# When an encoder kernel's weight sums are transferred: six spacings and one delay changed

## The chip, the cores and the metric

The kernel runs on one core of a Trainium2 chip. The metric is the device time of one execution in microseconds (us), given as the median of several runs. The core's engines each work through a queue of their own, in order: TensorE (PE in the profile; PEld is its weight loads) multiplies, VectorE (DVE) and ScalarE (ACT) work on elements, GpSimd (POOL) does small work and issues some DMAs, SyncE (SP) issues most of the DMAs. All DMAs of the core share 16 DMA engines.

## What is computed

Two encoder layers over 256 tokens and 16 meta tokens, 2048 channels, float32. Cut to what matters:

```python
for i in range(DEPTH):                                   # 2 layers
    proj = rmsnorm(x, norm_mix[i]) @ w_in[i]             # q | k | v | f | ga | gf
    a_br = attention(q, k, v) @ w_attn_br[i]
    fr = real(fft2(f, axes=(position, group channel)))   # 8 groups of 128 channels
    s_br = fr @ w_four[i]
    x = x + (sigmoid(ga) * a_br + sigmoid(gf) * s_br) @ w_out[i]
    up = rmsnorm(x, norm_ffn[i]) @ w_up[i]
    x = x + (silu(dwconv3(up[:, :D_FF])) * up[:, D_FF:]) @ w_down[i]
return x[:, 16:]
```

## The kernel before

**Weight blocks.** Weights come from memory in blocks of 512 KB (128 partitions, 4 x 256 columns). Each block is loaded by SP into one of four buffers `raw` (L244; six in the last layer's feed-forward), rounded by ACT into `wh` (L280), and the rest of the rounding is formed by DVE as `wl` (L283); `wh` and `wl` have three buffers each. A block takes 24 matmuls: for each of 8 column pieces wh by the high part of the activations, wh by the low part, wl by the high part (L352 to L354). In the first layer the Fourier branch's blocks are first folded by DVE into `wpm` (L271). The list `order` fixes the sequence of all blocks; `next_split` starts the loads some blocks ahead of use.

**Stages.** Per layer: projections f (first layer), k, v, q; in the last layer f comes folded, between the second and the third q group, with its own loop of 16 blocks (`folded_f`, matmuls at L822 to L826, tiles `ps_f`). Then the branches in two halves after `BRANCH_ORDER`: the gates ga0 to ga7 and gf0 to gf7 (4 blocks each), the Fourier products s0 to s7 and attention products a0 to a7 (2 blocks each). After each half comes a half of the output projection (`ps_o`, 16 blocks). Then the feed-forward: up (`ps_ug`, `ps_uv`) and down (`ps_d`).

**Weight sums.** In the last layer part of the up and of the down projection is computed with fewer matmuls, from sums and differences of weight blocks and of activations (`products`, L1390, 196 products of one block each, spread over the layer's 152 other blocks by the list `DUE`). The sums of weight blocks are made ahead, in DRAM, by DMAs that GpSimd issues: first a copy of 1 MB from one place to another (L539), then a second transfer of 1 MB that adds to it. These are 56 copies and 56 accumulating transfers, 112 in all, in a fixed order: the sums for the up projection (`fv`, 32 transfers), then those for the first and second set of the down projection (`ft`, 48 and 32). Within a set of n pairs the order is copy, copy, add, copy, add and so on to copy, add, add. Each transfer stands behind a small copy on GpSimd (`tick`, L538) that reads the `wl` made last, so that it can't start much ahead of the matmuls.

**Steps.** While blocks are multiplied, a function `step` is called four times a block (twice for a product's block, not in `folded_f`). It does two things: it counts down to the next weight-sum transfer, one every `slow[2]` steps (0: none), and it runs at most one pending small task from a list, each of which says for how many steps it then waits. `drain` runs everything in that list at once, whatever it still waits for.

```python
if not force and slow[1] and slow[2]:
    slow[0] -= 1
    if slow[0] <= 0:
        slow[0] = slow[2]
        if next(slow[1], None) is None:
            slow[1] = None
```

In steps the stages are: first layer from gf0 on, 160 for the first half of the branches, 64 for its output projection, 160 and 64 for the second, 1056 for the feed-forward; last layer 96 for k, v and q, 120 to the third gf (gf2), 104 for the rest of the first half, 64, 160 and 64, then 1000 for the feed-forward.

**The first Fourier projection.** The first layer's f groups run first: groups 0 and 1 together in 32 steps, group 2 in 16, then `drain`, then group 3. A task of norm sums runs beside them: sixteen squares from step 4 to step 28, the statistics at steps 32, 36, 40 and 42, and then `f_evac` of group 0 at step 45 and of group 1 at step 47. `f_evac` ends by putting `f_chan` of its group on the list (L636), whose small products are written to `ps_fa` (L652, L653).

**Who sets the order.** Within an engine the planner of the language orders instructions by the program's order and by when it reckons their inputs ready; where the code says so (`keep_in_program_order`, `manual_schedule`) the program's order holds. The ticks and transfers keep theirs.

Of the kernel before, what the change touches and what calls it, by code (L numbers as in the profile page):

```python
# [158 lines left out]
def encoder_kernel(ctx, tc, xT, params, consts, bmat, cfold, csign, w_fl, w_f64c, w_in, w_abr, w_four, w_f64, w_out, w_up, w_down, w_vn, w_dn, w_dt, out):  # L159
# [129 lines left out]
    def push(gen, wait=0):  # L289
        shadow.append([wait, gen])  # L290

    slow = [0, None, 0]
# [296 lines left out]
    for l in range(DEPTH):  # L589
        last = l == DEPTH - 1  # L590
# [5 lines left out]
        with tc.tile_pool(name=f"mix{l}", bufs=1) as mp:  # L596
# [17 lines left out]
            def rt(name):  # L614
                return mp.tile([P, 2, 2 * TH], F32, tag="r", name=name, bufs=7)[:, :, :T]
# [8 lines left out]
            def f_evac(i, ps):  # L624
                ft = rt("ft")
                for m in range(MG):
                    nc.vector.tensor_tensor(ft[:, m, :], ps[m][:, :T], rstdB, op=ALU.mult)
                g2 = slice(2 * i, 2 * i + 2)
                tt = nc.vector.tensor_tensor
                nc.vector.tensor_copy(E[:, g2, 0:1], ft[:, :, 0:1])  # L630
                tt(E[:, g2, 1:128], ft[:, :, 1:128], ft[:, :, 271:144:-1], op=ALU.add)
                tt(E[:, g2, 128:256], ft[:, :, 1:129], ft[:, :, 271:143:-1], op=ALU.subtract)
                tt(remE[:, g2, 0:8], ft[:, :, 128:136], ft[:, :, 144:136:-1], op=ALU.add)
                nc.vector.tensor_copy(remE[:, g2, 8:9], ft[:, :, 136:137])
                tt(remO[:, g2, 9:16], ft[:, :, 129:136], ft[:, :, 143:136:-1], op=ALU.subtract)
                push(f_chan(i), 11 if l == 0 and i == 1 else 8)  # L636

            def chan_out(i, pv):
                hh = o1[0][:, i]
# [514 lines left out]
            def gate(kind, i):  # L1154
                ps = group((l, kind, i), xr(lo), W)
                th = rt("th")
                boff = 2 * KT * l + (0 if kind == "ga" else KT)
                for m in range(MG):
                    u = th[:, m, lo:T]
                    nc.vector.tensor_tensor(u, ps[m][:, :W], rstdB[:, lo:T], op=ALU.mult)  # L1160
                    bcol = bgh[:, boff + 2 * i + m:boff + 2 * i + m + 1]
                    nc.scalar.activation(u, u, AF.Tanh, bias=bcol, scale=0.5)
                return th

            tha, thf, w64s = {}, {}, []
            for half in range(2):
                slow[2] = 0
                mH = mL = None
                for n_, (kind, i) in enumerate(BRANCH_ORDER[half]):
                    if half or n_ >= (8 if last else 4):  # L1170
                        slow[2] = 26 if last else 15
                    j = i - 4 * half
                    if kind == "ga":
                        tha[i] = gate("ga", i)
                    elif kind == "gf":
                        w64s.append(split_w64(l, i))
                        thf[i] = gate("gf", i)
                    elif kind == "s":
                        def s_evac(m, ps, th=thf[i]):
                            e, o = (mp.tile([P, TH], F32, tag=t, name=t) for t in ("se", "so"))  # L1180
                            for a, p_ in ((e, ps[0]), (o, ps[1])):
                                nc.scalar.copy(a, p_[:, TH:2 * TH])
                                nc.vector.tensor_tensor(a, p_[:, :TH], a, op=ALU.add)
                            sp = mp.tile([P, T], F32, tag="sp", name="sp", bufs=2)
                            nc.vector.tensor_tensor(sp[:, 0:TH], e, o, op=ALU.add)
                            nc.vector.tensor_tensor(sp[:, TH:T], e[:, T - TH:0:-1], o[:, T - TH:0:-1], op=ALU.subtract)
                            t_ = th[:, m, lo:T]
                            nc.vector.scalar_tensor_tensor(t_, t_, 1.0, sp[:, lo:T], op0=ALU.add, op1=ALU.mult)

                        four_group((l, "s", i), fr, x64, w64s.pop(0), s_evac)  # L1190
                    else:
                        if mH is None:
                            drain()
                            mHf = mp.tile([P, AHn], F32R, tag="aH", name="mH")
                            mLf = mp.tile([P, ALn], F32R, tag="aL", name="mL")
                            mH = mHf[:, :8 * T].rearrange("p (k t) -> p k t", k=8)
                            mL = mLf[:, :8 * T].rearrange("p (k t) -> p k t", k=8)
                        ps = group((l, "a", i), lambda kt: (qH[kt // 4][:, kt % 4, lo:T], qL[kt // 4][:, kt % 4, lo:T]), W)
                        for m in range(MG):
                            k = 2 * j + m  # L1200
                            t_, h_ = tha[i][:, m, lo:T], mH[:, k, lo:T]
                            nc.vector.scalar_tensor_tensor(t_, t_, 1.0, ps[m][:, :W], op0=ALU.add, op1=ALU.mult)
                            nc.vector.tensor_tensor(t_, t_, thf[i][:, m, lo:T], op=ALU.add)
                            nc.scalar.copy(h_, t_)
                            nc.vector.tensor_tensor(mL[:, k, lo:T], t_, h_.bitcast(F32), op=ALU.subtract)  # L1205
                slow[2] = 22 if last else 20 if half else 15
                for mg in range(8):
                    ps = group((l, "o", half, mg), lambda kt: (mH[:, kt, lo:T], mL[:, kt, lo:T]), W)
                    for m in range(MG):
                        mt = 2 * mg + m  # L1210
                        nc.vector.scalar_tensor_tensor(XT[:, mt, lo:T], ps[m][:, :W], 0.5, XT[:, mt, lo:T], op0=ALU.mult, op1=ALU.add)
                        if half == 1:
                            norm_in(mt, P_NF + l * KT)


        with tc.tile_pool(name=f"ffn{l}", bufs=1) as fp:
# [46 lines left out]
                            norm_in(mt, P_NM + (l + 1) * KT)  # L1263
                k0 += n
            if not last:
                slow[2] = 0

            if last:
                X0, X1 = 26, 32
# [102 lines left out]
                def products():  # L1372
                    late = []
                    until(hold, "tokens")
                    slow[2] = 45
                    make_ahead()
                    bank.extend([psum.tile([P, 512], F32, tag="aux", name=f"ps_p{i}{h}") for h in range(2)] for i in range(2))
                    for s_, p, q in PRODUCTS:
                        ps = bank[(p in (4, 2, 1)) ^ s_ % 2]
                        fresh = p in (0, 4, 1)  # L1380
                        wh, wl = (w.rearrange("p c m -> p (c m)") for w in next_split())
                        direct = s_ == 0 and p in plain
                        if direct:
                            k, h = plain[p]
                            a, b = xH[:, k + q, xt[h]], xL[:, k + q, xt[h]]
                        else:
                            a, b = made.pop((s_, p, q))
                        for x, w, first, end in ((a, wh, True, False), (b, wh, False, False), (a, wl, False, True)):
                            for h in range(2):
                                nc.tensor.matmul(ps[h], x, w[:, 512 * h:512 * h + 512], start=fresh and (s_, q) in BEGIN and first,  # L1390
                                                 stop=(s_, q) in END and end, skip_group_check=not fresh)
                            if not first:
                                step()
                                pump()
                        if not direct and units[used[0]][1][-1] == q:
                            used[0] += 1
                        make_ahead()
                        if late and q % 2 == 0:
                            hand_out(*late.pop(0))
                        if (s_, q) in END:  # L1400
                            while late:
                                hand_out(*late.pop(0))
                            t_, c, minus = {0: (0, 0, 0), 4: (1, 2, 0), 5: (0, 2, 1), 2: (0, 2, 0), 6: (1, 2, 1), 1: (0, 0, 0), 3: (1, 0, 0)}[p]
                            late += [(s_, p, t_, c + h, ps[h], minus) for h in range(2)]
                            if p in (0, 3) or s_ == 0 and p == 6:
                                while late:
                                    hand_out(*late.pop(0))
                        yield
                    assert not late

                slow[2] = 18
                st["products"] = products()
                st["pool"] = fp
                for i in UP_ORDER:
# [131 lines left out]
```

## Time and profile before

| | |
|---|---|
| median of 3 runs | 2542.79 us (2540.98 to 2543.11) |
| profiled execution | 2546.1 us |
| its span | 2544.3 us |
| granted TensorE clock, mean | 0.999 |
| TensorE busy | 2528.2 us |
| VectorE busy | 1825.0 us |
| ScalarE busy | 1319.8 us |
| DMA moved, mean | 660.69 MB, 260 GB/s |

The span runs from the first to the last instruction of one profiled execution; the execution's time adds what lies around it. Busy time is the time in which at least one instruction of an engine was in flight. Matmuls overlap, so a group of them can be slower than it should be without TensorE showing idle. A group's line gives the source line, engine, operation, the tiles written and read, the count, and the busy and mean times. In the views by stage each engine's busy time is followed by its count of instructions; the row ends in the granted clock, the DMA engines' share and GB/s. A window cut around one kind of tile counts the instructions that touch it, neighbours at its edges too.

### The profile page before, as it was taken

To read this page: it belongs to the slowest core of one execution; us is meant where nothing else is said; L and a number is where in the kernel's file an instruction comes from. 1 tells how busy PE (TensorE), PEld (TensorE's weight loads), DVE (VectorE), ACT (ScalarE), POOL (GpSimd) and SP (SyncE) were. 2 spreads that over 40 slices of the span, in tenths; PEclk is the share of its full clock that TensorE was granted. 3 is DMA by queue.
4 is the path that set the end of the run, shared out by engine and by line. 5 is a ranking of instruction groups with operands and counts; after the bars stand their busy time and mean duration, and the time that the engine had idled before them with its cause. 6 is when DMAs were issued, how large, how long until landed. Compare 5 with 4: busy or idle time off the path is not lost.

```text
span 2544.3 us, 47646 instructions
## 1 busy us (share of the span) xinstructions
PE 2528.2 (99%) x18992; PEld 2447.4 (96%) x18992; DVE 1825.0 (72%) x2889; ACT 1319.8 (52%) x1893; POOL 132.3 (5%) x265
## 2 busy tenths in 40 slices
PE   9999999999999999999999999999999999999999
PEld 8999999999999999999999999999988999888987
DVE  7687766776666556666558877666778778777788
ACT  5455434554444334444445555444676566656565
POOL 0000100000000000000000000000000000000000
PEclk9999999999999999999999999999999999999999
DMA  6546889989989998999875646887889888887787
GB/s 238 163 156 217 261 270 288 280 262 302 308 271 305 300 306 274 281 318 294 252 247 183 201 150 209 246 266 240 260 293 282 298 274 285 288 286 264 240 268 261
DMA packets 171215, 660.69 MB, mean 260 GB/s; under 512 B 19424, under 2 KB 24672, under 8 KB 170096
## 3 DMA queue, kind: packets, MB, share of 16 engines
q1 hardware_dynamic: 152528, 538.07, 61.3%
q0 software_dynamic: 17024, 117.45, 18.7%
q8 instruction: 149, 2.44, 0.4%
q10 hardware_dynamic: 1440, 2.13, 0.2%
q14 instruction: 74, 0.61, 0.1%
HBM read 635.91 MB, written 136.31 MB: 304 GB/s over the span
## 4 chain that ended last, share of the span: by engine, by line
PE 86%; DMA 2%; DVE 1%; ACT 1%; issue 0%; ACTq 0%; DVEq 0%
PE ps_p L1390 10%; PE ps_ug L353 7%; PE ps_ug L354 7%; PE ps_ug L352 7%; PE ps_uv L348 4%; PE ps_d L353 3%; PE ps_uv L353 3%; PE ps_d L352 3%; PE ps_uv L354 3%; PE ps_d L354 3%; PE ps_uv L352 3%; PE ps_o L353 2%; PE ps_o L354 2%; PE ps_o L352 2%; PE ps_uv L349 2%; PE ps_gf L354 2%
## 5 line engine op out<-in xcount | busy, mean ns | idle before, releaser
L283 DVE TENSOR_TENSOR wl<-raw,wh 128x1024 fp32r<-128x1024 f32 (+1 forms) x937 | 1129.7, 1217 | 567.5 <-ACT wh L280 559.5
L280 ACT CAST wh<-raw 128x1024 fp32r<-128x1024 f32 (+1 forms) x937 | 976.0, 1046 | 890.8 <-PE ps_ug L353 201.2
L353 PE MATMUL ps_ug<-xHL,wh 128*128 128x272 f32 (+1 forms) x1408 | 401.9, 285 | 0.0
L354 PE MATMUL ps_ug<-xHL,wl 128*128 128x272 f32 (+1 forms) x1408 | 401.4, 285 | 0.4 <-DVE wl L283 0.4
L352 PE MATMUL ps_ug<-xHL,wh 128*128 128x272 f32 (+1 forms) x1408 | 400.8, 285 | 0.0
L353 PEld LDWEIGHTS ps_ug<-xHL,wh 128*128 128x128 f32 x1408 | 264.7, 188 | 3.2
L352 PEld LDWEIGHTS ps_ug<-xHL,wh 128*128 128x128 f32 x1408 | 264.6, 188 | 3.2
L354 PEld LDWEIGHTS ps_ug<-xHL,wl 128*128 128x128 f32 x1408 | 264.7, 188 | 0.6 <-DVE wl L283 0.6
L353 PE MATMUL ps_uv<-xHL,wh 128*128 128x272 f32 x704 | 203.3, 289 | 0.0
L353 PE MATMUL ps_d<-gHL,wh 128*128 128x272 f32 x704 | 202.9, 288 | 0.0
L352 PE MATMUL ps_d<-gHL,wh 128*128 128x272 f32 x704 | 202.9, 288 | 0.0
L354 PE MATMUL ps_uv<-xHL,wl 128*128 128x272 f32 x704 | 202.6, 288 | 0.0
L352 PE MATMUL ps_uv<-xHL,wh 128*128 128x272 f32 x704 | 202.3, 287 | 0.0
L354 PE MATMUL ps_d<-gHL,wl 128*128 128x272 f32 x704 | 202.1, 287 | 0.0
L1390 PE MATMUL ps_p<-wh,opnd 128*128 128x512 f32 x688 | 187.8, 394 | 0.0
L348 PE MATMUL ps_uv<-xHL,wh 128*128 128x512 f32 x448 | 159.8, 395 | 0.0
L353 PE MATMUL ps_o<-mL,wh 128*128 128x272 f32 (+1 forms) x512 | 146.6, 286 | 1.3 <-DVE mL L1205 1.3
L352 PE MATMUL ps_ga<-xHL,wh 128*128 128x272 f32 (+1 forms) x512 | 147.8, 289 | 0.0
L352 PE MATMUL ps_gf<-xHL,wh 128*128 128x272 f32 (+1 forms) x512 | 146.9, 287 | 0.1
L354 PE MATMUL ps_gf<-xHL,wl 128*128 128x272 f32 (+1 forms) x512 | 146.0, 285 | 0.4 <-DVE wl L283 0.4
L353 PE MATMUL ps_ga<-xHL,wh 128*128 128x272 f32 (+1 forms) x512 | 146.1, 285 | 0.0
L353 PE MATMUL ps_gf<-xHL,wh 128*128 128x272 f32 (+1 forms) x512 | 146.1, 285 | 0.0
(372 smaller groups left out, 5871.4 us busy)
## 6 DMA issues: line engine op xcount, KB each, us to landing
raw<-in_w_up SPq DMA_DIRECT2D x320, 512.0 KB, 5.2
raw<-in_w_in SPq DMA_DIRECT2D x191, 512.0 KB, 4.2
raw<-in_w_down SPq DMA_DIRECT2D x88, 512.0 KB, 5.4
raw<-ft SPq DMA_DIRECT2D x80, 512.0 KB, 4.8
raw<-in_w_out SPq DMA_DIRECT2D x64, 512.0 KB, 5.6
ft<-in_w_dn POOLq DMA_DIRECT2D x30, 1024.0 KB, 12.0
raw<-in_w_dn SPq DMA_DIRECT2D x60, 512.0 KB, 4.7
raw<-in_w_abr SPq DMA_DIRECT2D x32, 512.0 KB, 4.8
```

Of the source, the lines that this page charges most:

```text
L280: nc.scalar.copy(h[:, a:b], r[:, a:b])
L283: nc.vector.tensor_tensor(lo[:, a:b], r[:, a:b], h[:, a:b].bitcast(F32), op=ALU.subtract)
L348: nc.tensor.matmul(o2, h[:, c, sl], ab, start=kt == 0, stop=False)
L349: nc.tensor.matmul(o, lo[:, c, sl], ab[:, 0, :], start=False, stop=kt == nk - 1)
L352: nc.tensor.matmul(o, h[:, c, sl], a, start=kt == 0, stop=False)
L353: nc.tensor.matmul(o, h[:, c, sl], b, start=False, stop=False)
L354: nc.tensor.matmul(o, lo[:, c, sl], a, start=False, stop=kt == nk - 1)
L1390: nc.tensor.matmul(ps[h], x, w[:, 512 * h:512 * h + 512], start=fresh and (s_, q) in BEGIN and first, stop=(s_, q) in END and end, skip_gr ...
```

## The change

The spacings `slow[2]` of the weight-sum transfers are set anew, and the wait of `f_chan` in the first layer is 10 steps for group 0 (8 before) and 13 for group 1 (11 before). By stage, the spacing in steps:

| stage | before | after |
|---|---|---|
| first layer, gf0 to the end of the first half, and its output projection | 15 | 32 |
| first layer, second half of the branches | 15 | 32 |
| its output projection and the first feed-forward | 20 | 19 |
| last layer, k to gf2 | none | 40 |
| last layer, rest of both halves of the branches | 26 | 26 |
| last layer, output projections | 22 | 28 |
| last feed-forward, to the first product | 18 | 28 |
| last feed-forward, from the first product | 45 | 38 |

```diff
-                push(f_chan(i), 11 if l == 0 and i == 1 else 8)
+                push(f_chan(i), (10, 13, 8, 8)[i] if l == 0 else 8)
...
             for half in range(2):
-                slow[2] = 0
+                slow[2] = (40 if half == 0 else 26) if last else 0 if half == 0 else 32
                 mH = mL = None
                 for n_, (kind, i) in enumerate(BRANCH_ORDER[half]):
-                    if half or n_ >= (8 if last else 4):
-                        slow[2] = 26 if last else 15
+                    if half == 0 and n_ == (8 if last else 4):
+                        slow[2] = 26 if last else 32
...
-                slow[2] = 22 if last else 20 if half else 15
+                slow[2] = 28 if last else 19 if half else 32
                 for mg in range(8):
...
             if not last:
-                slow[2] = 0
+                slow[2] = 40
...
                     until(hold, "tokens")
-                    slow[2] = 45
+                    slow[2] = 38
...
-                slow[2] = 18
+                slow[2] = 28
                 st["products"] = products()
```

## The prediction

> **What bounds the kernel now.** I read first the page's head and its busy line.
>
> ```profile
> span 2544.3 us, 47646 instructions
> PE 2528.2 (99%) x18992; PEld 2447.4 (96%) x18992; DVE 1825.0 (72%) x2889; ACT 1319.8 (52%) x1893; POOL 132.3 (5%) x265
> ```
>
> TensorE is busy for 2528.2 of 2544.3 us. The change takes no work from it, so all it can return is time in which TensorE waits. The next view, busy time by stage, says where that is.
>
> ```profile
> 250.00:310.00 60.00, 55.85 (x429) 54.85 (x428) 43.35 (x75) 26.09 (x40) 5.44 (x10) 0.97 0.87 264
> 560.00:1330.00 770.00, 770.00 (x6145) 770.00 (x6144) 477.49 (x697) 330.46 (x413) 47.21 (x103) 1.00 0.90 289
> 1420.00:1560.00 140.00, 140.00 (x1163) 138.63 (x1162) 112.09 (x267) 77.69 (x162) 3.83 (x4) 1.00 0.48 157
> 1700.00:1800.00 100.00, 98.70 (x825) 98.49 (x825) 67.09 (x108) 49.64 (x74) 4.66 (x10) 1.00 0.83 250
> 1850.00:1990.00 140.00, 139.29 (x824) 122.86 (x823) 109.93 (x135) 93.04 (x120) 6.31 (x10) 1.00 0.90 299
> 1990.00:2225.00 235.00, 235.00 (x1559) 215.70 (x1558) 188.23 (x252) 143.37 (x182) 11.41 (x16) 1.00 0.87 282
> ```
>
> After the stretch, its length and TensorE's busy time, the last three columns are granted clock, DMA share and GB/s. The idle sits in the first layer's branches (4.15 us at 250 to 310), with crumbs at 1700 (1.30) and 1850 (0.71). The first feed-forward (560 to 1330) has none, though its DMA engines are 0.90 busy.
>
> Busy time hides part of a loss, because overlapping matmuls fill in. So I set equal groups side by side: the attention products a0, a1, a2 and Fourier products s1, s3, s4 of the first layer, its gates gf5, gf6, and the last layer's two output projections.
>
> ```profile
> 250.60:256.80 6.20, 6.15 (x48) 6.04 (x48) 0.43 (x1) 1.00 0.69 238
> 273.80:284.20 10.40, 7.78 (x48) 7.58 (x48) 0.44 (x1) 0.84 0.53 164
> 300.30:306.80 6.50, 6.33 (x48) 6.05 (x48) 0.43 (x1) 1.00 1.24 462
> ```
>
> ```profile
> 256.70:261.40 4.70, 4.18 (x34) 3.97 (x34) 0.06 (x1) 0.44 (x2) 1.00 0.97 217
> 306.80:311.90 5.10, 4.26 (x34) 4.06 (x34) 0.14 (x1) 0.45 (x2) 1.00 0.35 134
> 378.50:382.50 4.00, 3.99 (x34) 4.00 (x34) 0.51 (x2) 0.45 (x2) 1.00 1.03 269
> ```
>
> ```profile
> 400.90:413.60 12.70, 12.32 (x96) 12.03 (x96) 0.01 (x1) 1.00 0.88 291
> 435.70:447.70 12.00, 12.00 (x96) 11.95 (x96) 0.00 (x0) 1.00 1.08 317
> ```
>
> ```profile
> 1627.00:1673.10 46.10, 46.10 (x384) 46.10 (x384) 6.35 (x15) 1.00 0.83 254
> 1781.20:1829.00 47.80, 46.50 (x384) 46.16 (x384) 6.35 (x15) 1.00 0.79 260
> ```
>
> Same work, different time: a1 loses 10.40 - 6.20 = 4.2, a2 0.3, s1 0.7, s3 1.1, together 6.3 us; gf5 loses 0.7; the second output projection 1.7. All told **8.7 us**.
>
> The chain of waits and GpSimd's timeline name the cause.
>
> ```profile
> 265.17 9.15 DMA raw<-in_w_four
> ...
> 1770.93 9.91 DMA raw<-in_w_out
> ...
> 1964.55 11.01 DMA raw<-in_w_up
> ```
>
> ```profile
> 255.38 0.88 POOL L539 DMA_DIRECT2D fv<-in_w_vn  x1
> ...
> 265.71 0.50 POOL L539 DMA_DIRECT2D fv<-in_w_vn  x1 [0.25 <-issue]
> ```
>
> ```profile
> 1768.66 0.89 POOL L539 DMA_DIRECT2D ft<-in_w_dn  x1 [0.26 <-issue]
> ```
>
> The first two late weight loads are in flight with weight-sum transfers, issued at 255.38 (an accumulation) and 265.71, and at 1768.66. Sizes and landings, first in the branches, then in the attention stage, where no sums run:
>
> ```profile
> raw<-in_w_in SPq DMA_DIRECT2D x18, 512.0 KB, 5.1
> ...
> fv<-in_w_vn POOLq DMA_DIRECT2D x4, 1024.0 KB, 10.8
> ...
> fv<-in_w_vn POOLq DMA_DIRECT2D x3, 7.0
> ```
>
> ```profile
> raw<-in_w_in SPq DMA_DIRECT2D x50, 512.0 KB, 3.5
> ```
>
> An accumulating transfer (the row with KB) is in flight 10.8 us, a copy 7.0; a weight load needs 3.5 us alone and 9 to 11 beside an accumulation. VectorE works in order: while wpm (L271) waits for the load of 265.17, the wl split behind it waits too, and a1 waits for that.
>
> **The change, part by part.** A step is six matmuls; 6145 matmuls in the 770 us of the first feed-forward make 0.75 us a step, so 15 steps are 11 us, shorter than or equal to an accumulation's flight: the next transfer starts before the last has landed. 32 steps are 24 us. Counting four steps a weight block, the 112 transfers fall as follows, before and after: first branches and first output projection's half, 26 and 12; rest of the first layer (19 for 20), 56 and 59; last layer's projections to its third gf, 0 and 6 (one each 40); its remaining branches and output projections, 16 and 14; its feed-forward, 14 and 21, of which 11 for 8 accumulate. No work is added: each carries the same tick copy and launch, only later.
>
> *First branches.* The launch of 255.38 is that of step 61. At 32 steps they come at steps 1, 33, 65, 97 and 129, so at about 234, 258, 282 and 306 us. The pair that held the load of 265.17 becomes one accumulation at 258, landed by 269; a copy at 282 lands at 289, and nothing is in flight with the loads for s1 and s3, issued some 10 us ahead of 256.7 and 306.8. I take 6.0 of 6.3 back. If another load pays instead, it is 0 at worst, since fewer transfers are in flight at any time; 6.3 is the top. In the second half the accumulation at s4 stays (step 225, before 226), but those beside it go, so gf5 gives 0.4 of 0.7.
>
> *The clock.* Part of a1's 4.2 us is this:
>
> ```profile
> 278.00:281.20 3.20, 3.20 (x16) 3.20 (x16) 1.99 (x4) 1.88 (x3) 0.06 (x1) 0.50 0.93 275
> ```
>
> After the wait the granted clock is 0.50 for 3.2 us, which costs 1.6 us more. The Trainium skill, TensorE: Matmul & The Clock Gate, section "What's actually happening", has the gate close only after an idle window of about 3.4 us. By that rule a wait as short as this (at most 2.6 us of idle in a1's row) would leave the clock alone, and the sum would be 1.6 us smaller; the trace differs, so the measured loss stands in my sum.
>
> *Last layer's output projections, 22 to 28.* The accumulation at 1768.66 gives way to a copy at step 532, 12 steps before the second projection, so near 1772, beside the same loads: in flight 7.0 instead of 10.8 us. I take half of 1.7, 0.85; the bounds are 0, where the copy holds the loads as long, and 1.7 back.
>
> *Six new transfers in the last layer's attention stage.* The stage from 1420 has room, 157 GB/s, and TensorE 140.00 of 140. The lean place is the folded Fourier projection:
>
> ```profile
> 1386.00:1420.00 34.00, 33.95 (x293) 33.26 (x292) 30.42 (x45) 23.24 (x37) 0.25 (x2) 1.00 0.80 245
> ```
>
> ```profile
> L244 SPq DMA_DIRECT2D raw<-fw x5: 320/332/536, 1371.8 to 1382.7; - x5
> ```
>
> VectorE is busy 30.42 of 34 us there. The stage's first matmul comes at step 64 of the layer; the second new launch, an accumulation, falls at step 42, 22 steps or 16 us ahead, near 1369, and is in flight until 1380. The stage's first five loads are issued from 1371.8 on, the first of them 14 us ahead of use, so most of it is covered; uncovered it would cost 11.0 - 3.5 = 7.5 us. A gain is excluded: there is 0.05 us of idle to gain. I take 1.0, nearer to nothing because it lands some 6 us before the first folded matmul. On GpSimd's queue six ticks and launches, 0.9 us each by the launch rows, now stand among the power operations (L493) that the attention statistics wait for, and a tick itself waits for a wl split; three such operations, one launch late each, would be 2.7 us, but the attention's matmuls wait for nothing in the 1420 row, so I take 0. What frees the wl buffer is the tick, and three buffers cover one launch.
>
> *19 for 20.* Fifty-six transfers cost no idle in 560 to 1330; 59 get 0. Bounds: 0 (no idle to gain) and 30 accumulations at 0.35 (half of 0.71, the two waits in the 1850 row), 10.5.
>
> *Last feed-forward, 28 and 38 for 18 and 45.* Fourteen transfers cost 0.71 there; 21 at that rate cost 1.07, so 0.3 more. Its launches, three 28 steps apart and 18 more at 38, end at step 6 + 56 + 684 = 746 of 1000; the products that read the last sums are the last eight of 196, past step 950, so no load on SP's queue waits for a sum. Bounds: -0.7, and 14 (11 accumulations at the 1.30 of the 1700 row).
>
> *Fourier products two steps later.* I cost this at nothing, since it does nothing: the evacuations that start the two waits come at steps 45 and 47, the group ends at step 48, and the drain there runs everything pending whatever its wait.
>
> ```profile
> 4.30:44.56 40.26, 39.61 (x288) 37.97 (x288) 0.78 (x2) 0.00 (x0) 1.00 0.85 291
> ```
>
> ```profile
> 44.58 0.33 PE L652 MATMUL ps_fa<-cst,E 128*128 128x65 f32 x2
> ```
>
> The 288 ps_f matmuls are all of the first three groups; ps_fa comes right behind them, at the drain. Waits of 8 or 10, 11 or 13 end there alike.
>
> **Sum.** -6.0 - 0.4 - 0.85 + 1.0 + 0.3 = **-5.9 us**. The profiled execution took 2546.1 us, a span of 2544.3 and 1.8 around it; the span becomes 2538.4. The median of the runs is 2542.79, 3.3 under the profiled one; I subtract the same: **2536.9 us**, 0.23% less.
>
> **Rivals.**
> *The wait moves to the folded projection.* The 7.5 us bound comes in full: 2542.79 - 7.25 + 7.5 + 0.3 = 2543.3. For it, VectorE's 30.42 of 34 us; against it, the 14 us of lead.
> *The timed runs have less to give back.* If the 3.3 us that the profiled execution is longer are such waits, 8.7 shrinks to 5.4, the 7.25 recovered to 4.5, and 1.3 of new cost leaves 3.2: 2539.6. For it, 2.1 us between the fastest and slowest run; against it, nothing in the rows.
> *The last feed-forward becomes the bound (slower).* Place: from 1860 on, where products take a 512 KB block each and the DMA share is already 0.90. Price: 1.30 for each of 11 accumulations instead of 0.71 for all, 13.6 more: 2542.79 - 6.25 + 13.6 = 2550.1. It turns the sign from 0.63 us an accumulation on, where 11 of them eat the 6.25 that is left and the 0.71. Against it: 235.00 of 235 us busy from 1990 on, accumulations and all.
> *The spacing changes nothing* (2542.8): if loads wait for each other, not for the sums; the 3.5 against 9.15 speaks against it.
>
> **How the numbers follow.** Forecast 0.46; the wait moves 0.16; less to give 0.17; nothing changes 0.04; last feed-forward 0.17. This kernel's measurement tells about 0.2%, 5.1 us, from no change: below 2537.7 is faster, above 2547.9 slower. Faster holds the forecast and nothing of the rest, 0.46; the three middle cases are within, 0.37; slower 0.17. The range runs from 2532.5 (all 8.7 and the 0.71 back, 2533.4, and half of the 1.8 by which the fastest run lies under the median) to 2545.0 (the moved wait and the same 1.8 above it); it leaves out the last rival. The forecast's own range is 2533.4 to 2538.5.
>
> **What would show it.** Right: the stretch 250 to 310 busy above 59.5 us at clock 1.00, a1 near 6.2, launches 24 us apart, an output projection under 47.2; the stretch of the folded projection still within 0.5 us; last launch some 180 us ahead of the end; ps_fa behind 288 ps_f. Wrong: idle in the first feed-forward, in the folded projection, or more than 2 us of it between 1860 and 2400.

## The result, and the profile after

The changed kernel takes **2546.89 us** (median of 20 runs, 2541.09 to 2551.55) against 2542.16 us for the kernel before (20 runs, 2540.98 to 2547.67): 4.7 us more, ratio 1.0015, 95% interval 1.0008 to 1.0022. The interval excludes 1, so the kernel became slower, though by less than the 0.2% taken as no change. The forecast was 2536.9 and the range ended at 2545.0, so both are missed.

The profiled execution of the changed kernel took 2548.88 us, 2.0 above its median; that of the kernel before lies 3.9 above the median of these 20 runs. The page of the changed kernel begins:

```profile
span 2547.1 us, 47654 instructions
PE 2530.6 (99%) x18992; PEld 2449.7 (96%) x18992; DVE 1824.9 (72%) x2889; ACT 1318.1 (52%) x1893; POOL 132.7 (5%) x265
```

The same 18992 matmuls keep TensorE busy for 2.4 us more than before, in a span 2.8 us longer. Where that is shows in busy time by stretch, the same six stretches as before the change:

```profile
250.00:310.00 60.00, 59.86 (x478) 59.30 (x477) 47.49 (x83) 30.82 (x49) 3.10 (x6) 1.00 0.71 223
560.00:1330.00 770.00, 770.00 (x6144) 769.93 (x6143) 476.23 (x696) 330.05 (x412) 52.66 (x107) 1.00 0.90 291
1420.00:1560.00 140.00, 139.84 (x1161) 138.43 (x1160) 111.53 (x267) 76.76 (x160) 7.48 (x12) 1.00 0.56 179
1700.00:1800.00 100.00, 100.00 (x838) 100.00 (x838) 68.06 (x111) 49.74 (x76) 5.29 (x12) 1.00 0.79 251
1850.00:1990.00 140.00, 138.46 (x814) 121.50 (x813) 109.27 (x134) 91.75 (x118) 7.64 (x12) 1.00 0.89 296
1990.00:2225.00 235.00, 233.40 (x1550) 213.93 (x1550) 187.89 (x252) 142.73 (x182) 9.62 (x16) 1.00 0.86 290
```

The first layer's branches have given their idle back (59.86 of 60 us busy, 55.85 before), the second output projection too (100.00 of 100 at 1700). The first feed-forward is as full as it was. The last feed-forward lost 1.54 us at 1850 and 1.60 at 1990, where it had lost 0.71 and nothing.

A stretch with fixed ends slides over the work, so the table below uses lengths of stages: from the start of a stage's first matmul to the start of the next stage's, worked out from the start times in the two traces.

| stage, us | before | after | difference |
|---|---|---|---|
| first layer's f groups | 56.2 | 58.6 | +2.4 |
| first layer, first half of the branches from gf0 on | 125.2 | 118.9 | -6.3 |
| its output projection, second half, output projection | 210.2 | 209.0 | -1.2 |
| first feed-forward | 795.0 | 795.2 | +0.1 |
| last layer, folded Fourier projection | 33.6 | 38.0 | **+4.4** |
| third q group, then gates and the rest of the first half of the branches | 207.4 | 209.0 | +1.6 |
| second output projection | 47.7 | 46.2 | -1.6 |
| last feed-forward, to its tail | 667.4 | 670.9 | **+3.5** |

The first row is no part of the change's effect: TensorE runs the same instructions there in the same order in both kernels, and the kernels below that share this part with the changed one, instruction for instruction, take between 54.9 and 60.3 us for it. The stages left out differ by 0.1 or less. So 9.1 us were gained, and 9.6 lost, chiefly at two places. In this pair of profiles the change therefore costs 0.5 us, where the medians differ by 4.7: the profile of the kernel before is a slow one of its kind, and so overstates what there was to gain. The part on the prediction comes back to this.

**The folded projection.** Busy time of the instructions that touch `ps_f`, in the kernel before and in the changed one (the last three columns are granted clock, DMA share and GB/s):

```profile
1380.00:1420.00 40.00, 33.75 (x288) 33.02 (x288) 1.02 (x4) 1.17 (x6) 1.00 0.79 244
```

```profile
1380.00:1425.00 45.00, 35.29 (x288) 34.50 (x288) 2.02 (x8) 2.04 (x9) 0.96 0.72 237
```

The same 288 matmuls are in flight 1.5 us longer, at a clock of 0.96. Two short stretches of the changed kernel, all instructions, show the hole and what followed it:

```profile
1382.00:1386.00 4.00, 1.14 (x11) 0.92 (x10) 3.20 (x5) 1.86 (x3) 0.00 (x0) 1.00 0.05 18
1386.00:1390.00 4.00, 4.00 (x22) 3.92 (x23) 1.94 (x5) 1.22 (x2) 0.00 (x0) 0.57 0.69 233
```

TensorE idles for 2.86 of 4 us, and then runs for 4 us at 0.57 of its clock, which is another 1.7 us: together 4.6, about the +4.4 of the table. During the hole the DMA engines are at 0.05: almost nothing is being carried any more, the lateness is older. GpSimd's timeline, and then the chain of waits, of the changed kernel:

```profile
1366.54 0.95 POOL L539 DMA_DIRECT2D ft<-ft  x1 [0.30 <-issue]
```

```profile
1373.87 0.60 SPq L902
...
1375.79 5.21 DMA qs<-qp
1381.00 0.02 issue
1381.02 0.72 DVE qs L906
...
1384.55 1.23 DVE wl L283
1385.79 0.04 issue
1385.83 0.33 PE ps_f L826
```

At 1366.54 the second of the six new transfers starts, an accumulation; it lands 10.3 us later. SP issues four small DMAs from 1373.87 on: the half swaps (L902, 68 KB each) that the rotary step of the last layer's first q group reads. The DMA groups of 1364 to 1392, before and after, give the size and the median time to landing:

```profile
qs<-qp SPq DMA_DIRECT2D x4, 68.0 KB, 2.3
```

```profile
qs<-qp SPq DMA_DIRECT2D x4, 68.0 KB, 5.9
```

VectorE's timeline, first before, then after, with its idle time ahead of the instruction in brackets:

```profile
1382.96 0.73 DVE L906 TENSOR_TENSOR qs<-qs,cst 128x544 f32<-128x544 f32 x1 [0.27 <-DMA qs<-qp]
```

```profile
1381.02 0.72 DVE L906 TENSOR_TENSOR qs<-qs,cst 128x544 f32<-128x544 f32 x1 [3.38 <-DMA qs<-qp]
...
1384.55 1.22 DVE L283 TENSOR_TENSOR wl<-raw,wh 128x1024 fp32r<-128x1024 f32 x1
```

In this part VectorE keeps the program's order. It stands at L906 for 3.38 us, and the `wl` split that the folded matmuls wait for stands behind it. The weight block of that split was in time: it landed at 1377.00, and ScalarE had rounded it by 1379.23.

How the accumulation reached the swaps shows in the landings, taken from the two traces (issued, landed, us):

| transfer | before | after |
|---|---|---|
| accumulation | none | 1366.54, 1376.80 |
| weight block, two ahead of the swaps | 1374.95, 1378.13 | 1369.88, 1377.00 |
| weight block, one ahead of the swaps | 1377.87, 1381.32 | 1372.80, 1380.00 |
| first swap | 1378.94, 1381.70 | 1373.87, 1380.31 |
| last swap | 1380.86, 1382.94 | 1375.79, 1381.00 |

SP's transfers land in the order of their issue: in none of the twelve profiles does one of the 1084 loads and copies on its queue land ahead of one issued before it. A block issued during the accumulation landed 0.2 us after it, the next 3.0 us later, and the swaps 0.3 us behind that one. So the swaps stood in a queue behind held blocks; the blocks had the time to wait, the swaps had not.

**The last feed-forward.** TensorE's waits from 1850 to 2450, before and after:

```profile
PE ps_ug L354 <- DVE wl L283: 0.4, 1, 0.4
PE ps_uv L349 <- DVE wl L283: 0.3, 1, 0.3
```

```profile
PE ps_ug L354 <- DVE wl L283: 1.6, 2, 1.3
PE ps_uv L349 <- DVE wl L283: 1.1, 2, 0.8
PE ps_p L1390 <- DVE wl L283: 0.3, 1, 0.3
```

Two of the waits have an accumulation behind them. GpSimd's timeline shows the launches; ScalarE's shows it idle for a load 13.7 us after the second launch:

```profile
1860.02 0.95 POOL L539 DMA_DIRECT2D ft<-in_w_dn  x1
...
2069.81 0.89 POOL L539 DMA_DIRECT2D ft<-in_w_dn  x1 [0.32 <-issue]
```

```profile
1861.54 9.99 DMA raw<-in_w_vn
```

```profile
2083.47 1.05 ACT L280 CAST wh<-raw 128x1024 fp32r<-128x1024 f32 x1 [2.13 <-DMA raw<-in_w_up]
```

The load of 1861.54 is in the chain of waits, 9.99 us long; the chain goes on through two roundings and splits to a matmul at 1877.16 that waited 0.77 us. The accumulation of 2069.81 landed at 2083.19 and the load that ScalarE waits for at 2083.37. TensorE notices at 2092, when VectorE has still not caught up, and waits 1.31 us ahead of 2093.86.

TensorE runs its 18992 matmuls in the same order in both kernels, so each can be set beside its counterpart. The changed kernel falls back by 1.4 us from 1871 to 1882, by 0.6 from 1948 to 1952 and by 2.1 from 2087 to 2097, and it is spared 0.7 near 1980, where the kernel before had waited for a load: together the 3.5 of the table.

### The profile page after: what moved, and what is told of

Its sections match the earlier page's. It is cut to its first block, busy times and chain, and to the rows that moved or that the text cites. A ratio compares the mean times of both kernels' runs of the same rounds, so it can differ in the third digit from the quotient of the medians.

```text
span 2547.1 us, 47654 instructions
## 1 busy us (share of the span) xinstructions
PE 2530.6 (99%) x18992; PEld 2449.7 (96%) x18992; DVE 1824.9 (72%) x2889; ACT 1318.1 (52%) x1893; POOL 132.7 (5%) x265
## 4 chain that ended last, share of the span: by engine, by line
PE 93%; DVE 3%; DMA 2%; ACT 1%; issue 0%; SPq 0%; POOL 0%; ACTq 0%; DVEq 0%; POOLq 0%
PE ps_p L1390 10%; PE ps_ug L353 7%; PE ps_ug L354 7%; PE ps_ug L352 7%; PE ps_uv L348 4%; PE ps_d L353 3%; PE ps_uv L353 3%; PE ps_d L352 3%; PE ps_uv L354 3%; PE ps_d L354 3%; PE ps_uv L352 3%; PE ps_o L353 2%; PE ps_o L352 2%; PE ps_o L354 2%; PE ps_gf L352 2%; PE ps_gf L353 2%
## 5 line engine op out<-in xcount | busy, mean ns | idle before, releaser
L354 PE MATMUL ps_o<-mH,wl 128*128 128x272 f32 (+1 forms) x512 | 146.1, 285 | 0.0
## 6 DMA issues: line engine op xcount, KB each, us to landing
ft<-in_w_dn POOLq DMA_DIRECT2D x30, 1024.0 KB, 11.7
```

The costliest lines, as they stand in the source:

```text
L354: nc.tensor.matmul(o, lo[:, c, sl], a, start=False, stop=kt == nk - 1)
```

## The experiments

Ten runs, with the kernel before on the same chip beside them. **Theory 1**: the loss is the folded projection, through the swaps. **Theory 2**: it is the last feed-forward. **Theory 3**: it is the closer spacing (19 for 20) of the first feed-forward. The last two runs name theories of their own. "Difference" is the median less that of the kernel before in the same batch (2543.49 in the first, 2543.1 in the second, 2543.5 in the third); the stages are of the profiled execution, measured as in the table above.

| run | difference, us | ratio, 95% interval | folded projection | last feed-forward |
|---|---|---|---|---|
| the change (above) | +4.7 | 1.0015 (1.0008 to 1.0022) | 38.0 | 670.9 |
| no_qk | -4.8 | 0.9982 (0.9974 to 0.9991) | 33.6 | 667.7 |
| late_rope | -0.3 | 0.9997 (0.9988 to 1.0006) | 34.2 | 669.7 |
| first_layer | -1.9 | 0.9993 (0.9984 to 1.0002) | 33.6 | 666.6 |
| one_add | +6.4 | 1.0023 (1.0014 to 1.0033) | 37.2 | 4.0 over before |
| ffn45 | +6.0 | 1.0020 (1.0011 to 1.0029) | 37.5 | 669.5 |
| ffn_shift | +1.2 | 1.0001 (0.9992 to 1.0010) | 37.4 | 666.7 |
| real_delay | -0.5 | 0.9999 (0.9990 to 1.0007) | 33.6 | as before |
| best1 | -5.3 | 0.9979 (0.9970 to 0.9988) | 33.6 | 2.4 over before |
| mended | -2.3 | 0.9990 (0.9981 to 0.9999) | 34.4 | 666.8 |

**no_qk: the changed kernel without transfers from k to the first gates.** The six transfers go between ga0 and gf2 instead, 20 steps apart.

```diff
-                slow[2] = (40 if half == 0 else 26) if last else 0 if half == 0 else 32
+                slow[2] = (20 if half == 0 else 26) if last else 0 if half == 0 else 32
...
             if not last:
-                slow[2] = 40
+                slow[2] = 0
```

> The changed kernel, with no weight-sum transfer during k, v and q of the last layer; the same six stand between ga0 and gf2, one each 20 steps. Theory 1 (the accumulation in flight at 1366.5 holds the query's half swaps, VectorE waits 3.4 us for them in order, TensorE waits 3.0 us and then runs 3.5 us at half clock): the folded projection falls from 38.0 to about 33.6 us, and the time from 2546.9 to about 2542.5. Theory 2 (the loss is in the last feed-forward, 3.5 us more there in the profile of the change): the time stays within 1 us of 2546.9, and the feed-forward keeps its waits. Theory 3 (19 for 20 in the first feed-forward): no difference.

Measured: 2538.69 us, ratio 0.9982; 8.2 us under the changed kernel by the medians, 9.5 by the differences. The `ps_f` row:

```profile
1370.00:1425.00 55.00, 33.76 (x288) 33.02 (x288) 2.02 (x8) 2.02 (x9) 1.00 0.72 226
```

33.76 us at full clock, as before the change. The last feed-forward fell by 3.1 us as well, though none of its lines was edited: other steps of the countdown put its transfers elsewhere. So this run shows that the six transfers' place decides the sign, but by itself not through which of the two stages.

**late_rope: the changed kernel with the swaps' use put off.** All transfers stay; the rotary step of the last layer's first q group comes 5 steps later, so that VectorE reaches L906 after the swaps have landed.

```diff
-                yield 6 - j
+                yield 11 if last and i == 0 else 6 - j
```

> The changed kernel, with all its transfers where they are; only the step in which VectorE takes up the swapped halves of the last layer's first q group comes 5 steps, 3.7 us, later. Theory 1: the swap has landed by then, VectorE's wait of 3.38 us falls under 0.5 and the folded projection to 34 to 35 us; the time falls by 3 to 4.4 us, to 2542.5 to 2544. If instead the weight loads held by the accumulation were to blame, VectorE waits as long at the next wl split, and nothing is gained. Theories 2 and 3: no difference.

Measured: 2543.16 us, ratio 0.9997. This is the test of theory 1 alone: the accumulation is still there (launched at 1365.73) and still slows the swaps, but VectorE doesn't wait:

```profile
1379.61 0.72 DVE L906 TENSOR_TENSOR qs<-qs,cst 128x544 f32<-128x544 f32 x1
...
1444.49 0.73 DVE L906 TENSOR_TENSOR qs<-qs,cst 128x544 f32<-128x544 f32 x1 [2.66 <-DMA qs<-qp]
```

The folded projection takes 34.2 us, so 3.8 of the 4.4 are back. The second line is a wait of the same kind, for the third q group's swaps, 2.66 us where the changed kernel waits 0.58. In both kernels a copy of the six is launched 0.6 us ahead of them; here it is in flight for 8.9 us (from 1434.65), in the changed kernel for 5.8 (from 1439.26).

**one_add: the kernel before with one accumulation at step 42 of the last layer.**

```diff
             if not last:
-                slow[2] = 0
+                slow[0], slow[2] = 42, 1000
...
+                    if last and half == 0 and n_ == 8:
+                        slow[0] = 7
                     if half or n_ >= (8 if last else 4):
```

> The kernel before, with one accumulating transfer moved from the last feed-forward to step 42 of the last layer, where the change has one; all else as before. Theory 1: this transfer alone costs what the folded projection lost in the change, 4.4 us (3.0 of wait and 1.4 of half clock): 2545 to 2547. Theories 2 and 3: within 1 us of 2542.2.

Measured: 2549.88 us, ratio 1.0023. One transfer in that place makes the kernel before slower than the whole change does. Folded projection 37.2 us, and the `ps_f` row shows the hole and the clock again:

```profile
1370.00:1425.00 55.00, 35.32 (x288) 34.52 (x288) 2.02 (x8) 2.04 (x9) 0.97 0.81 244
```

The other 4.0 us are in the last feed-forward, with the spacings of before (18 and 45): moved by one in the sequence, an accumulation came at 1854.4, where a copy had been launched.

**first_layer: the kernel before with the first layer's branches at 32 steps.** Its first feed-forward has 16 instead of 20, so that the other stages keep their transfers.

```diff
-                        slow[2] = 26 if last else 15
+                        slow[2] = 26 if last else 32
...
-                slow[2] = 22 if last else 20 if half else 15
+                slow[2] = 22 if last else 16 if half else 32
```

> The kernel before, with the first layer's branches at 32 steps alone, and the transfers that this leaves over put into its second output projection and feed-forward, at 16 steps instead of 20 (70 transfers there, not 56); the last layer as before. Theory 1 or 2: the branches give their 7.5 us and nothing is paid: 2535 to 2537, ratio to before about 0.997. Theory 3: at 16 steps, closer than the 19 of the change, the first feed-forward shows idle of TensorE of several us, and the time is not under 2541.

Measured: 2541.58 us, ratio 0.9993, not the 0.997 of theories 1 and 2 and not told apart from no change. The branches took 120.3 us, 4.9 less than before; the first feed-forward took 805.7 instead of 795.0 in the profiled execution, which at 2550.03 us was the slowest of the eleven.

**ffn45: the changed kernel with 45 steps in the last feed-forward again.**

```diff
-                    slow[2] = 38
+                    slow[2] = 45
```

> The changed kernel with 45 steps, as before, for 38 between the transfers of the last feed-forward; its accumulation near 1860 us, where the products begin, stays. If the spacing is what cost the 3.5 us of the last feed-forward (ug to the tail 667.4 us before, 670.9 in the change), it falls to about 667.5 and the time by 3 us, to about 2544. If the place of single accumulations is what costs, the wait near 1875 stays at 1.3 us and the stage stays above 669.

Measured: 2549.12 us, ratio 1.0020, no better than the change. The feed-forward takes 669.5 us, 1.4 less than in the change and still 2.1 over before; one_add, with the spacings of before, lost 4.0 there. So the closer spacing is not what costs the most of it.

**ffn_shift: the changed kernel with the last feed-forward's transfers 20 steps later.** Spacing as in the change.

```diff
-                slow[2] = 28
+                slow[0], slow[2] = slow[0] + 20, 28
                 st["products"] = products()
```

> The changed kernel with all transfers of the last feed-forward 20 steps later, spacings as changed, so that the accumulation of 1860 falls near 1872. If places decide: the wait near 1875 is gone, the stage falls below 669 (other places may pay), the time falls by 1.5 to 3 us. If the spacing decides: the stage stays at 670 to 671, the time within 1 us of the change's.

Measured: 2544.32 us, ratio 1.0001. In the changed kernel the accumulation came at 1860.02, as the products begin; here it comes at 1872.25, and TensorE's waits from 1850 to 2450 shrink to

```profile
PE ps_uv L349 <- DVE wl L283: 0.3, 1, 0.3
```

The same number of accumulations, at the same spacing, costs 4.2 us less. The folded projection keeps its loss (37.4). Theory 2 holds for a part of the loss, and what decides is where single accumulations fall.

**real_delay: the kernel before with a wait for `f_chan` that takes effect.** The planned order of instructions is the same in every engine whether the diff's 10 and 13 or the old 8 and 11 stand in the line, since `drain` runs what is pending. Here the drain ahead of group 3 is replaced by a wait for the evacuations only.

```diff
-                push(f_chan(i), 11 if l == 0 and i == 1 else 8)
+                push(f_chan(i), (10, 13, 8, 8)[i] if l == 0 else 8)
...
                         f_evac(i, pss[i])
                         yield 2
+                    hold["evac"] = True
...
                     ps = group((l, "f", 2), xr(0), T, "aux")
-                drain()
+                until(hold, "evac")
```

> The kernel before with the waits of 10 and 13 steps for the small Fourier products, and with the drain behind group 2 replaced by a wait for the two evacuations alone, so that these waits are not cut short. The first stage (to the first k matmul) took 54.9 to 58.6 us in the five profiles, whose order of instructions there is one and the same, with 1.2 us of idle before ps_fa and in one of them half clock behind it. If that wait is what varies, the stage is 54 to 55 us, and the time falls by 1 to 2.5 us below before, with a narrower spread. If the variation is in the first loads, nothing changes.

Measured: 2542.58 us, ratio 0.9999. The products do move, from 45 to 50 us on (changed kernel, then this one):

```profile
L652 PE MATMUL ps_fa<-cst,E x16: 218/275/417, 45.2 to 69.5; 128*128 128x65 f32 x16
```

```profile
L652 PE MATMUL ps_fa<-cst,E x16: 218/275/275, 50.7 to 67.4; 128*128 128x65 f32 x16
```

The wait of 1.1 us ahead of them in the profile of the kernel before is not in this profile, but nor is it in that of no_qk, where they come at the old place. Moved in earnest, they change nothing that can be measured.

**best1: no_qk and real_delay together.**

> no_qk and the true delay of real_delay together: 2538.7 less what real_delay gives, 2536.5 to 2538, ratio to before 0.9975 or under.

Measured: 2537.81 us, ratio 0.9979 (0.9970 to 0.9988): the best of all, 5.3 us under the kernel before, though short of the 0.9975 expected and not told apart from no_qk.

**mended: the changed kernel with late_rope's and ffn_shift's edits.**

> The changed kernel with both repairs at once: the half swaps of the last layer's first q group put 5 steps later, and the transfers of the last feed-forward 20 steps later, all six transfers of the attention stage kept. Theory 1 (the loss is made of two single places, the swaps held by the accumulation at 1366 and the weight load held by the one at 1854): the two gains found apart, about 3.7 and 3.5 us, add up, so some 7 us under the changed kernel, near 2539.5, ratio to the kernel before near 0.9985; folded projection 34 us, last feed-forward near 667. Theory 2 (loads and sums share what the DMA engines move, so a wait mended at one place comes back at another): the gains overlap and the ratio stays between 0.9995 and 1.0005, with the folded stage or the feed-forward still 2 us or more above the kernel before.

Measured: 2541.21 us, ratio 0.9990; 5.7 us under the changed kernel by the medians, 7.0 by the differences. The gains nearly add up, and the two mended stages are short, 34.4 and 666.8 us. (The launch at 1854 of the expectation is one_add's; in the changed kernel it is the one at 1860.02.) So mending these two places is enough to undo the slowdown: the same number of transfers, six of them still in the attention stage, then gives 2.3 us. But theory 2 has its part, for in the profiled execution the wait in the third q group grew. GpSimd's timeline, then VectorE's:

```profile
1437.73 0.56 POOL L539 DMA_DIRECT2D ft<-in_w_dn  x1 [0.25 <-issue]
```

```profile
1448.92 0.73 DVE L906 TENSOR_TENSOR qs<-qs,cst 128x544 f32<-128x544 f32 x1 [4.00 <-DMA qs<-qp]
```

The next of the six transfers, a copy, was launched half a microsecond ahead of that group's swaps and was in flight for 8.6 us; VectorE waited 4.00 us, and TensorE 2.6 for the roundings and splits behind it.

**first_layer_again: first_layer profiled once more.**

> The kernel before with the first layer's spacings alone, profiled once more. Its profile so far shows 805.7 us for the first feed-forward against 795.0 in the kernel before, while its median was 1.9 us under the kernel before. Theory A (the waits there are of that one execution): this time the first feed-forward takes 795 to 799 us and the execution 2539 to 2543. Theory B (a spacing of 16 steps in the first feed-forward holds weight loads in every execution): waits for wh again near 601 and 644 us, the first feed-forward above 803 us.

Measured: one execution, 2547.33 us, first feed-forward 804.5 us. The chain of waits and GpSimd's timeline:

```profile
627.18 13.47 DMA raw<-in_w_up
```

```profile
621.42 0.89 POOL L539 DMA_DIRECT2D fv<-in_w_vn  x1 [0.25 <-issue]
630.73 0.52 POOL L539 DMA_DIRECT2D fv<-in_w_vn  x1 [0.26 <-issue]
```

TensorE's waits near 644 and 735 are in both profiled executions, that near 603 only in the first, and the stage is above 803 us in both, so theory B in the main: at 16 steps, some 12 us and at times 9, the copy of 630.73 starts before the accumulation of 621.42 has landed, and a load issued between them takes 13.47 us. Theory 3 is answered from the other side: at 19 steps the changed kernel's row 560 to 1330 is full, at 16 it is not. Whether the unprofiled runs of first_layer, 2538.86 to 2544.11 us, had the wait as well stays open.

## Why the prediction was wrong

- **The bound** was right: TensorE, with idle only in named places. The range's upper end should read 2545.1 by its own sum (2543.3 + 1.8), which changes nothing.
- **First branches, -6.0:** right in the profile, -6.3. Launches came 23 us apart, at 236.76, 259.85, 282.75 and 305.46, and a1 took its 6.1 us at full clock:

```profile
275.00:281.10 6.10, 6.02 (x48) 6.07 (x48) 0.44 (x1) 1.00 0.68 230
```

- In the timed runs it is probably less. Two profiles of kernels that leave these branches alone, one_add and real_delay, have 123.2 and 123.4 us there, against 125.2 in the profile before. So 4.4 us is as good a figure, and the rival "less to give back" had that much in it.
- **Gate gf5 and output projections, -0.4 and -0.85:** right in kind, too small. The stages gave 1.2 and 1.6; the second output projection is now

```profile
1781.95:1828.20 46.25, 46.15 (x384) 46.22 (x384) 5.93 (x15) 1.00 0.75 241
```

- **The six new transfers, +1.0: this step failed.** It placed the accumulation well (launch near 1369, landed by 1380; it was 1366.54 and 1376.8) and looked at the right stage, but took the weight blocks for what it would hold up, and their lead of 14 us for cover. The blocks were held and covered, as it said. Uncovered were four transfers of 68 KB queued behind them with no lead at all: VectorE comes to them as soon as they can be there, 0.27 us of wait already before. They were in flight 3.6 us longer, and in VectorE's fixed order that became 2.9 us of TensorE wait and 1.7 us of half clock. late_rope shows it: with the accumulation left in place and only the reader put off, 3.8 us come back. The bound of 7.5 held, and the rival "the wait moves to the folded projection" had the place, at a price of 7.5 where 4.4 was measured.
- **The last feed-forward, +0.3: mis-sized,** measured +3.5. The mean over 14 transfers was no price for the next seven: most accumulations cost nothing, and three places cost 1.4, 0.6 and 2.1 us. The slower rival had the place (from 1860 on) and the size per transfer, but not for all 11 accumulations, and ffn_shift shows that their position costs, ffn45 that the spacing is at most a small part.
- **The new transfers beyond the folded projection, 0:** the 1420 row lost only 0.16 us, but the stages from the third q group to the first output projection grew by 1.6. Matmul by matmul, 1.0 of it comes at 1606 to 1613, behind a load issued at 1594.20, 2.4 us after an accumulation, that took 10.30 us; the stage varies by about as much on its own, 208.6 and 207.7 us in the two profiles of first_layer. In the mended kernel a copy there cost 2.6 us of wait, again through the swaps.
- **19 for 20, 0**, and **the last launch** (2367.84, 179 us ahead of the end): right. **Fourier products, 0**: right, since the edit changes no order.

With 4.4 for 1.0, 3.5 for 0.3, 1.6 for 0, and the gains as large as the profiles have them, the predicted sum of -5.9 becomes +0.5; the medians moved by +4.7. A part of the gains was not there in most executions. Against the profile that the forecast read, one_add and real_delay have 1.9 us less in the first branches, and real_delay, whose last layer is as before, 0.5 less in the second output projection. That takes the +0.5 to +2.9. The last 1.8 us are not placed.

## What to carry to other kernels

Before a background transfer is put into a stage that has room, list every load that an in-order engine reads there, with its lead: the victim here was the one with the least lead, small as it was, and what was ahead of it in its queue made it late. A mean cost per transfer hides that most cost nothing and some cost microseconds; move the launches by a few steps and look again before blaming their number. And a hole of 2 us or more on TensorE is to be priced with the slower clock behind it: 1.7 us each time here.

## What the runs showed of the hardware

A load issued while an accumulation is in flight tends to land right behind it. In the changed kernel's profile the accumulations were in flight for 11.7 us in the median, and behind 44 of the 56 a weight block issued meanwhile landed within 0.4 us of the accumulation; behind the 56 copies, none did. The first block to land behind an accumulation had taken 9.3 us in the median. So most accumulations hold some load, and yet most cost nothing; where one did cost, the held load, or what stood behind it on SP's queue, had too little lead.

Size does not protect a transfer. The swaps of 68 KB in the third q group had no held block ahead of them, since it had landed at 1442.05 in the changed kernel and at 1440.54 in the mended one; they landed 0.2 us after the copy launched ahead of them (1445.20 after 1445.01, and 1446.48 after 1446.29).

The clock can go down after a short idle. In the changed kernel TensorE waited 1.3 us ahead of the small Fourier products, and then ran like this, until 52 us; the stretch behind the wait of 1.1 us at the same place in the kernel before is the second row.

```profile
48.30:52.00 3.70, 3.70 (x20) 3.70 (x20) 3.45 (x16) 0.76 (x4) 0.00 (x0) 0.54 0.38 137
```

```profile
48.10:51.50 3.40, 3.40 (x29) 3.40 (x29) 3.28 (x13) 1.37 (x5) 0.00 (x0) 1.00 0.36 105
```

The Trainium skill, TensorE: Matmul & The Clock Gate, section "What's actually happening", asks for an idle window of about 3.4 us. These traces differ: all five idles of TensorE of 2.0 to 2.9 us in the twelve profiles, once it had started, were followed by half clock, and 7 of the 16 idles of 1.0 to 1.9 us. In the changed kernel the one of 1.3 us above was, and one of 1.3 us ahead of 2093.86 was not. Each time the clock stayed at half for 3.41 us or for twice that. The length of the idle alone doesn't decide; what does, no run here shows.
